# Splitting two projection weights once, in token block 2, for the last phase of a hybrid decoder block

## The chip, the core and the metric

The kernel runs on one core of a Trainium2 chip. The metric is the time of one execution in microseconds on the device, the median of several runs. A profile is one further execution, taken by the hardware profiler. The engines are TensorE (PE; its weight loads are PEld), VectorE (DVE), ScalarE (ACT), GpSimd (POOL) and SyncE (SP), which here issues the DMAs as one queue in order.

## What is computed

One decoder block on 2048 tokens of width 1024. An input projection feeds two branches, a causal convolution and an RWKV-7 recurrence; both are projected (`w_conv_out`, `w_rwkv_out`), merged by gates and projected once more (`w_out`).

```python
h = _rmsnorm(x, norm_g[l]) * (1.0 + scale[:, None, :]) + shift[:, None, :]
p = jnp.einsum('bsd,de->bse', h, w_in[l])
c_val, c_gate, c_og, ts, r_og, g_conv, g_rwkv = jnp.split(p, SPLITS, axis=-1)
y_conv = _conv_branch(c_val, c_gate, c_og, ..., w_conv_out[l])      # ... @ w_o
y_rwkv = _rwkv7_branch(ts, r_og, ..., w_rwkv_out[l])                # ... @ w_o
m = jax.nn.sigmoid(g_conv) * y_conv + jax.nn.sigmoid(g_rwkv) * y_rwkv
out = jnp.einsum('bsd,de->bse', m, w_out[l])
x = x + gate[:, None, :] * out
return _rmsnorm(x, final_g)
```

## The kernel before

The tokens are cut into four blocks of 512, the channels into eight tiles of 128. Every large matmul is made of three: a float32 operand is split into a high part (rounded to the type fp32r) and a low part (the rest), and the products high x high, high x low and low x high are summed (`mm3k`, L185). So each weight tile of 128 x 1024 (512 KB) is needed as two tiles of 512 KB.

`load_w` (L162) brings such a pair into the pool `w` of six buffers. If the pair is kept in DRAM, two DMAs fetch it (L168, L169). If not, the raw tile is loaded into a third buffer (L172), ACT casts it to the high part (L175), and DVE or POOL subtracts (L177). Pairs named in `KEPT`, the tiles of `w_in`, are then stored to DRAM for the later blocks (L181, L182). The last phase's output weight `w_o` is prepared apart: `ogate` (L147), called in token block 1, two weights in each of four groups, multiplies half a tile by the gate (POOL, L156), casts it (ACT, L157), subtracts (POOL, L158) and stores both halves (SP, L160). It works in the pool `hx` (L318), seven buffers of 128 x 512, which the normalisation of the next block's x (`xnorm`, L321) uses too, and with it the reading of the next block's input (`hprep`, L356).

The program has two parts. The first runs over the blocks (L859) and in each over four groups of heads: `group` (L560) holds the recurrence, with a triangular solve on POOL (L609, L611), its transposes on DVE (L637), the matmuls that read them (L641) and the state chain (L668 to L683); `conv` and `gates` (L746, L765) give PE projections to fill the chain's waits. The second part, the last phase, runs over the blocks again (L1030): `rproj` (L956) and `cproj` (L942) project the branches with w_ro and w_co through `project` (L733) and so `load_w`, eight tiles each and block; these 64 loads are raw, with `wcount[0] = -1000` (L964) giving their subtractions to DVE. Between them stand the output projection (L1059 to L1061), the next block's branch preparation (`osplit`, L927) and layer norm (`lnorm`, L984, whose statistics run L995, L1005, L1016 and whose values run L1024, L200 to L202, L1026, L912), and `finish` (L1071), the final norm with its run of one-column operations in `rsqrt` (L125 to L130).

The order on each engine is set by a scheduler that simulates the program when it is built (`schedule_with_timeline_sim`, L1135); `tc.high_priority` moves a few instructions ahead. On the chip each engine runs its own list in order.

Of the kernel before, what the change touches and what calls it, by code (L numbers as in the profile page):

```python
# [9 lines left out]
F32 = mybir.dt.float32  # L10
F32R = mybir.dt.float32r
I32 = mybir.dt.int32
AF = mybir.ActivationFunctionType
ALU = mybir.AluOpType
# [4 lines left out]
P = 128  # L19
D = 1024  # L20
KT = D // P
# [26 lines left out]
def lplan(t):  # L48
    n = {"c": 0, "g": 0}
    r = []  # L50
    for part in t.split():
        l = []
        for w in part:
            if w != "-":
                l.append(("1234" if w == "g" else w, n[w]))
                n[w] += 1
        r.append(l)
    return r
# [24 lines left out]
def hybrid_block(ctx: ExitStack, tc: tile.TileContext, x, vecs, convk, w2a2, final_g, ada, w_in, w_co, w_ro, w_o, crow, out,  # L83
                 seq=2048, groups=(0, 1, 2, 3), phase2=True, dbg=None):
    nc = tc.nc
# [6 lines left out]
    dp = ctx.enter_context(tc.tile_pool(name="dp", bufs=1, space=DRAM))  # L92
# [43 lines left out]
    wsrc = {"in": w_in, "co": w_co, "ro": w_ro, "o": {(cb, kh): w_o[cb, kh] for cb in range(4) for kh in range(2)}}  # L136
# [6 lines left out]
    kept = {}  # L143
# [3 lines left out]
    def ogate(n, half):  # L147

        back = kept.setdefault(("o", n), [dp.tile([P, KT, P], F32R, name=f"k{p_}_o{n[0]}_{n[1]}", tag=f"k{p_}_o{n[0]}_{n[1]}")
                                          for p_ in "hl"])  # L150
        hs = slice(half * 4, half * 4 + 4)
        st, gr, hi, lo = hx("w_st"), hx("w_gr"), hx("w_hi"), hx("w_lo")
        nc.sync.dma_start(st.rearrange("p (k n) -> p k n", k=4), wsrc["o"][n][:, hs, :])
        nc.sync.dma_start(gr[:, :256], grow_d[n[0] * 256:n[0] * 256 + 256].unsqueeze(0).broadcast_to([P, 256]))
        s4 = st.rearrange("p (k n) -> p k n", n=256)
        nc.gpsimd.tensor_tensor(out=s4, in0=s4, in1=gr[:, :256].unsqueeze(1).broadcast_to([P, 2, 256]), op=ALU.mult)  # L156
        nc.scalar.copy(hi.bitcast(F32R), st)  # L157
        nc.gpsimd.tensor_tensor(out=lo.bitcast(F32R), in0=st, in1=hi, op=ALU.subtract)  # L158
        for d_, s_ in zip(back, (hi, lo)):
            nc.sync.dma_start(d_[:, hs, :].bitcast(F32), s_.rearrange("p (k n) -> p k n", k=4))  # L160
# [152 lines left out]
    for g in range(4):  # L313
        s_ = c1.tile([P, 2, P], F32, name=f"S{g}")
# [3 lines left out]
    def hx(name):  # L318
        return xp.tile([P, TB], F32, name=name, tag="hx")

    def xnorm(b, tts=range(NTT)):  # L321
        for tt in tts:
            t0 = b * TB + tt * P
            ss = e2.tile([P, 8], F32, name="ss")
            xh = []
            for half in range(2):
                xt = hx("xt")
                nc.sync.dma_start(xt, x[t0:t0 + P, half * TB:half * TB + TB])
                nc.scalar.activation(hx("xsq"), xt, AF.Square, accum_out=ss[:, half:half + 1])
                xh.append(xt)  # L330
            vs, rs = ss[:, 2:3], ss[:, 3:4]
            nc.vector.tensor_tensor(out=vs, in0=ss[:, 0:1], in1=ss[:, 1:2], op=ALU.add)
            nc.vector.tensor_scalar(out=vs, in0=vs, scalar1=1.0 / D, scalar2=RMS_EPS, op0=ALU.mult, op1=ALU.add)
            rsqrt(rs, vs, e2, nc.vector, ss[:, 4:5])
            for kh in range(2):
                nc.vector.tensor_scalar(out=xh[kh], in0=xh[kh], scalar1=rs, scalar2=None, op0=ALU.mult)
                pt = pl.tile([P, 4, P], F32, name="late", tag="late")
                for i in range(4):
                    nc.tensor.transpose(pt[:, i, :], xh[kh][:, i * P:(i + 1) * P], ident)
                xo = hx("xTs").rearrange("p (a b) -> p a b", a=4)  # L340
                for i in range(4):
                    k = kh * 4 + i
                    nc.scalar.activation(xo[:, i, :], pt[:, i, :], AF.Identity, scale=g_col[:, k:k + 1],
                                         bias=shift_col[:, k:k + 1])
                nc.sync.dma_start(xT_dram[b][:, kh * 4:kh * 4 + 4, tt * P:(tt + 1) * P], xo)
# [10 lines left out]
    def hprep(b):  # L356
        h = ([], [])
        for k in range(KT):
            hf = hx("hf")
            nc.sync.dma_start(hf, xT_dram[b][:, k, :])  # L360
            hsplit(h, k, hf)
        return h
# [458 lines left out]
    def z_first(js):  # L821
        for j in js:
            z, bt = hx("z"), hx("zb")
            nc.sync.dma_start(z, o_dram[0][j])
            nc.sync.dma_start(bt, bv_dram[0][j])
            nc.gpsimd.tensor_tensor(out=z, in0=z, in1=bt, op=ALU.add)
            rt = hx("zr")
            nc.sync.dma_start(rt, ro_dram[0][j])
            nc.gpsimd.tensor_tensor(out=z, in0=z, in1=rt, op=ALU.mult)
            nc.sync.dma_start(z_dram[j], z)  # L830

    def lora_split(h):

        lf, ll, lx = hx("lora"), hx("lora_lo"), hx("lora_x")
        shifted(h, T_LORA, lf)
        nc.scalar.activation(lf[0:64], lf[0:64], AF.Tanh)
        lw = e1.tile([P, TB], F32R, name="lw", tag="lw")
        la = e1.tile([P, TB], F32R, name="la", tag="la")
        lo_, hi_ = slice(0, 64), slice(64, 128)
        for dst, sl, os_ in ((lw, lo_, hi_), (la, hi_, lo_)):  # L840
            nc.scalar.copy(dst[sl], lf[sl])
            nc.vector.tensor_tensor(out=ll[sl], in0=lf[sl], in1=dst[sl].bitcast(F32), op=ALU.subtract)
            nc.sync.dma_start(lx[os_], ll[sl])
            nc.scalar.copy(dst[os_], lx[os_])
        return lw, la
# [3 lines left out]
    def ada_steps():  # L849
        for k, _ in enumerate(ada_cols(srow, l3, "As", ASB, [((k, 8 + k), (mod[:, k:k + 1], mod[:, 8 + k:9 + k]))  # L850
                                                             for k in range(KT)])):
            ks, gs = slice(k, k + 1), slice(8 + k, 9 + k)
            nc.vector.tensor_tensor(out=shift_col[:, ks], in0=mod[:, ks], in1=ab[:, ks], op=ALU.add)
            nc.vector.tensor_tensor(out=g_col[:, ks], in0=mod[:, gs], in1=ab[:, gs], op=ALU.add)
            nc.vector.scalar_tensor_tensor(out=g_col[:, ks], in0=g_col[:, ks], scalar=1.0, in1=vc("norm_g", k),
                                           op0=ALU.add, op1=ALU.mult)
            yield

    for b in range(NB):  # L859
        h = hprep(b) if b else hprep0(x0, ada_steps())  # L860
        lora = lora_split(h)
        for g in groups:
            if b + 1 < NB:
                xnorm(b + 1, XN[g])
            else:
                z_first(ZN[g])
                if g < 3:
                    lnorm_first(g)
            if b + 1 < NB:
                todo = [(w, 2 * g + m) for w, m in (FIRST if b == 0 and g == 0 else NEXT)]  # L870
            else:
                todo = [wj for i in range(g, 4 if g < 3 else 5) if i == g or g == 3 for wj in lplan(LP)[i]]

            if b == 1:
                for _ in range(2):
                    n_ = later.pop(0)
                    for half in range(2):
                        ogate(n_, half)

            def fill(step, n=None):  # L880
                for _ in range(n or (FILL0[step] if b == 0 and g == 0 else 0)):
                    w, j = todo.pop(0)
                    if w == "c":
                        conv(b, h, j)
                    else:
                        gates(b, h, j, w)

            wcount[0] = WSH
            group(b, g, h, lora, fill)
            if b == 0 and g == GG:  # L890
                for _ in ada_cols(srow, l3, "As", ASB, [((16 + k, 17 + k), (hgate_col[:, k:k + 1], hgate_col[:, k + 1:k + 2]))
                                                        for k in range(0, KT, 2)]):
                    pass
                nc.vector.tensor_tensor(out=hgate_col, in0=hgate_col, in1=ab[:, 16:24], op=ALU.add)
                nc.vector.tensor_scalar(out=hgate_col, in0=hgate_col, scalar1=0.5, scalar2=None, op0=ALU.mult)
                nc.sync.dma_start(grow_d.rearrange("(n p) -> p n", p=P), hgate_col)
            wcount[0] = WDVE
            if todo:
                fill(0, len(todo))
# [75 lines left out]
    hl = ctx.enter_context(tc.tile_pool(name="hl", bufs=1, reuse_waits="tile"))  # L975
# [54 lines left out]
    for b in range(NB):  # L1030
# [7 lines left out]
        for tt in range(NTT):  # L1038
            xh = []
            for half in range(2):  # L1040
                n = 2 * tt + half
# [97 lines left out]
```

## Time and profile before

| | us |
|---|---|
| median of 3 runs (3077.19 to 3084.64) | 3080.32 |
| the profiled execution | 3079.25 |
| its span | 3077.6 |
| PE busy in the span | 2918.8 |
| DVE, ACT, POOL busy | 2182.2, 1059.7, 1161.0 |

Matmuls are pipelined, so PE's busy time counts overlapping operations once; where PE is not busy, it waits. A row of a group of instructions gives its line, engine, operation, the tiles (out<-in), the count, and durations. In a row of stretches of time (start:end, length) come the busy time of PE, PEld, DVE, ACT and POOL, each with the number of instructions in brackets, then the clock granted to PE as a share of full speed, the mean busy share of the 16 DMA engines, and GB/s.

### The profile page before, as it was taken

Reading aid. Unit: us, or ns where it says so; the run is one execution under the profiler, and the core shown is the slowest. Engines: PE = TensorE matmul, PEld = TensorE weight load, DVE = VectorE, ACT = ScalarE, POOL = GpSimd, SP = SyncE. Lnnn points to the kernel's source line nnn. Section 1 sums busy time; section 2 is a strip of 40 time slices with the busy share of each in tenths; the row PEclk is TensorE's granted clock in tenths of the full one; section 3 lists DMA queues with packets and bytes.
Section 4 is the critical chain, followed back from the end, with each engine's and each line's share of the span. In section 5 each row is a group of like instructions: output and inputs, shape, how many; then the busy total and the mean of one; then the engine's idle time right before and its main releaser. Section 6 shows DMA issues by size and latency. Waiting matters only on the chain.

```text
span 3077.6 us, 64859 instructions
## 1 busy us (share of the span) xinstructions
PE 2918.8 (95%) x25672; PEld 2759.5 (90%) x25672; DVE 2182.2 (71%) x4199; ACT 1059.7 (34%) x1919; POOL 1161.0 (38%) x1724
## 2 busy tenths in 40 slices
PE   6799998999999999999999999999989999699998
PEld 5789998999999999999999998999989888487888
DVE  7677877787777667777768586867699465877553
ACT  4424444343324241424232323233342224343421
POOL 3355554534343434241323326345445016533100
PEclk9989999999999999999999999999989999799999
DMA  8675767664757586555646567647448658766554
GB/s 301 221 239 192 262 206 268 229 235 136 249 160 229 163 269 218 178 167 173 204 149 217 181 202 247 192 142 224 139 146 263 207 187 287 246 205 220 198 182 161
DMA packets 343327, 638.41 MB, mean 207 GB/s; under 512 B 133424, under 2 KB 152176, under 8 KB 343024
## 3 DMA queue, kind: packets, MB, share of 16 engines
q1 hardware_dynamic: 343024, 634.27, 62.8%
q8 instruction: 202, 3.31, 0.4%
q14 instruction: 101, 0.83, 0.1%
HBM read 462.10 MB, written 170.92 MB: 206 GB/s over the span
## 4 chain that ended last, share of the span: by engine, by line
PE 62%; DVE 12%; DMA 10%; POOL 7%; issue 3%; ACT 2%; SPq 2%; DVEq 0%; POOLq 0%; ACTq 0%
PE ps_main L192 43%; PE aux L524 3%; DVE acc L761 2%; DMA w_st<-w_in_t 2%; POOL TT L611 2%; POOL itmp L609 2%; PE xo L673 2%; PE pout L1061 2%; PE pout L1060 2%; PE pout L1059 2%; DMA w_lo<-kl_in 1%; PE xo L668 1%; DMA w_gr<-grow_d 1%; PE xo L679 1%; PE late L695 1%
## 5 line engine op out<-in xcount | busy, mean ns | idle before, releaser
L192 PE MATMUL ps_main<-h_hi,w_hi 128*128 128x256 f32 x4608 | 961.4, 286 | 20.4 <-ACT w_hi L175 12.2
L192 PE MATMUL ps_main<-h_hi,w_lo 128*128 128x256 f32 x4608 | 962.3, 286 | 13.6 <-POOL w_lo L177 8.0
L192 PE MATMUL ps_main<-h_lo,w_hi 128*128 128x256 f32 x4608 | 956.7, 285 | 0.0
L192 PEld LDWEIGHTS ps_main<-h_hi,w_hi 128*128 128x128 f32 x4608 | 721.7, 190 | 30.4 <-ACT w_hi L175 13.3
L192 PEld LDWEIGHTS ps_main<-h_hi,w_lo 128*128 128x128 f32 x4608 | 719.7, 190 | 21.6 <-POOL w_lo L177 10.0
L192 PEld LDWEIGHTS ps_main<-h_lo,w_hi 128*128 128x128 f32 x4608 | 719.8, 190 | 5.2 <-issue 0.5
L761 DVE SCALAR_TENSOR_TENSOR acc<-u,ck,acc 128x512 f32<-128x512 f32 x928 | 698.6, 753 | 20.0
L175 ACT CAST w_hi<-w_st 128x1024 fp32r<-128x1024 f32 x135 | 141.5, 1048 | 368.9 <-DMA w_st<-w_in_t 151.6
L683 DVE SCALAR_TENSOR_TENSOR S<-xo,pe,Se 64x64 f32<-64x64 f32 x512 | 144.6, 282 | 128.1 <-PE xo L679 118.1
L609 POOL TENSOR_TENSOR itmp<-La,TT 128x126 f32<-128x126 f32 (+22 forms) x496 | 180.7, 364 | 141.9 <-DMA La<-dA 105.9
L611 POOL TENSOR_TENSOR TT<-TT,itmp 128x126 f32<-128x126 f32 (+22 forms) x496 | 190.5, 384 | 37.2
L177 DVE TENSOR_TENSOR w_lo<-w_st,w_hi 128x1024 fp32r<-128x1024 f32 x88 | 119.5, 1359 | 103.7 <-ACT w_hi L175 47.7
L177 POOL TENSOR_TENSOR w_lo<-w_st,w_hi 128x1024 fp32r<-128x1024 f32 x47 | 113.5, 2414 | 134.5 <-ACT w_hi L175 109.0
L665 ACT ACTIVATE Se<-S,pe 128x128 f32<-128x128 f32 x256 | 89.0, 395 | 209.1 <-DVE S L683 208.0
L524 PE MATMUL aux<-KR,BKz 128*128 128x128 f32 x1024 | 138.5, 285 | 13.5 <-ACT BKz L518 8.7
L547 POOL TENSOR_TENSOR vv<-rk,vv 128x512 f32<-128x512 f32 x32 | 44.0, 1374 | 284.2 <-ACT rk L546 268.8
L524 PEld LDWEIGHTS aux<-KR,BKz 128*128 128x128 f32 x1024 | 127.6, 198 | 16.1 <-ACT BKz L518 9.1
L675 DVE TENSOR_TENSOR uv<-xo,rn 64x256 f32<-64x256 f32 x128 | 53.7, 420 | 99.8 <-PE xo L673 98.2
L741 ACT ACTIVATE th<-ps_main 128x512 f32<-128x512 f32 x64 | 38.1, 595 | 210.5 <-PE ps_main L192 157.6
L526 DVE TENSOR_TENSOR As<-aux,maskA 128x512 f32<-128x512 f32 x128 | 87.0, 688 | 27.9 <-PE aux L524 26.4
L451 POOL TENSOR_TENSOR wlo<-wf,wl 64x128 fp32r<-64x128 f32 x64 | 37.4, 584 | 173.6 <-ACT wl L448 171.1
L773 ACT ACTIVATE th<-ps_main 128x512 f32<-128x512 f32 x64 | 38.2, 597 | 184.3 <-PE ps_main L192 179.7
(298 smaller groups left out, 5489.0 us busy)
## 6 DMA issues: line engine op xcount, KB each, us to landing
w_hi<-kh_in SPq DMA_DIRECT2D x219, 512.0 KB, 4.0
w_lo<-kl_in SPq DMA_DIRECT2D x219, 512.0 KB, 5.1
w_st<-w_in_t SPq DMA_DIRECT2D x73, 512.0 KB, 5.0
kh_in<-w_hi SPq DMA_DIRECT2D x71, 512.0 KB, 2.9
kl_in<-w_lo SPq DMA_DIRECT2D x71, 512.0 KB, 4.4
w_st<-w_ro_t SPq DMA_DIRECT2D x32, 512.0 KB, 4.0
w_st<-w_co_t SPq DMA_DIRECT2D x32, 512.0 KB, 3.6
w_hi<-kh_o SPq DMA_DIRECT2D x32, 512.0 KB, 3.7
```

Source lines behind the costliest of these rows:

```text
L175: nc.scalar.copy(hi, st)
L177: lo_eng.tensor_tensor(out=lo, in0=st, in1=hi.bitcast(F32), op=ALU.subtract)
L192: nc.tensor.matmul(ps[:, qs], ww[:, k, :], aa[k][:, qs], start=(k == 0 and t == 0 and q == 0), stop=(k == KT - 1 and t == 2 and q == ms - ...
L524: nc.tensor.matmul(pA[:, c // 2, es], BKz[:, hh, c // 2, es], KR[:, cc, es], start=(c == 0), stop=(c == 3), skip_group_check=True)
L526: nc.vector.tensor_tensor(out=Asb[:, hh, c4 * 4:c4 * 4 + 4, :].rearrange("p (a e) n -> p a (e n)", e=2), in0=pA, in1=flat(maskA).unsqueeze ...
L609: nc.gpsimd.tensor_tensor(out=tmp[:, :ni, :nt], in0=La[:, j:j + 1, j + 1:].broadcast_to([P, ni, nt]), in1=TT[:, :ni, j:j + 1].broadcast_to ...
L611: nc.gpsimd.tensor_tensor(out=TT[:, :ni, j + 1:], in0=TT[:, :ni, j + 1:], in1=tmp[:, :ni, :nt], op=ALU.add)
L665: nc.scalar.mul(Se[:, q, :], Sg[:, q, :], R[q]["pe"][:, c:c + 1])
L673: nc.tensor.matmul(xo[pr_, q, hs], As[q][pr_, hh, c, kcol(e)], XO[pr_, c, q, hs], start=(q == 0 and hh == 0), stop=(q == 1 and hh == 1), s ...
L683: nc.vector.scalar_tensor_tensor(out=Sg[hs, q, hs], in0=xo[hs, 2 + q, hs], scalar=R[q]["pe"][hs, c:c + 1], in1=Se[hs, q, hs], op0=ALU.mult ...
L761: nc.vector.scalar_tensor_tensor(out=acc if i + 1 < HALO else yj, in0=u[:, i:i + TB], scalar=ck[:, j, i:i + 1], in1=acc, op0=ALU.mult, op1 ...
L1059: nc.tensor.matmul(o_, mhi[kk][:, ts_], whi[:, k, :], start=first, stop=False, skip_group_check=True)
```

## The change

`keep` is `ogate` without the gate: half a raw tile of w_ro or w_co is loaded, cast on ACT, subtracted on POOL and stored as two halves in DRAM. It is called in token block 2, in every group for four of the sixteen tiles. `load_w` then finds the pair and fetches it, in all four blocks of the last phase.

```diff
+    pending = [(name, n) for name in ("ro", "co") for n in range(KT)]
+
+    def keep(name, n, half):
+        back = kept.setdefault((name, n), [dp.tile([P, KT, P], F32R, name=f"k{p_}_{name}{n}", tag=f"k{p_}_{name}{n}")
+                                           for p_ in "hl"])
+        hs = slice(half * 4, half * 4 + 4)
+        st, hi, lo = hx("w_st"), hx("w_hi"), hx("w_lo")
+        nc.sync.dma_start(st.rearrange("p (k n) -> p k n", k=4), wsrc[name][n][:, hs, :])
+        nc.scalar.copy(hi.bitcast(F32R), st)
+        nc.gpsimd.tensor_tensor(out=lo.bitcast(F32R), in0=st, in1=hi, op=ALU.subtract)
+        for d_, s_ in zip(back, (hi, lo)):
+            nc.sync.dma_start(d_[:, hs, :].bitcast(F32), s_.rearrange("p (k n) -> p k n", k=4))
...
+            if b == 2:
+                for _ in range(4):
+                    n_ = pending.pop(0)
+                    for half in range(2):
+                        keep(*n_, half)
```

Lines of the changed kernel are 13 higher from L162 on (18 from L880 on); the text uses the numbers of before. 64 casts of 128 x 1024 leave ACT and 64 subtractions leave DVE; 32 casts of 128 x 512 come to ACT and 32 subtractions to POOL. On SP, 64 loads of 512 KB are replaced by 128, and 96 DMAs of 256 KB come in.

The scheduler orders block 2 and all that follows anew. SP in block 2, group 3, before; dA and La carry the input of the triangular solve, kh_in and kl_in are kept w_in tiles:

```order
L168 DMA w_hi<-kh_in_7782 128x1024
L169 DMA w_lo<-kl_in_7783 128x1024
L595 DMA dA<-As 32x4x32 x8
L548 DMA bv_d_7_122<-vv 128x512
L168 DMA w_hi<-kh_in_7845 128x1024
L600 DMA La<-dA 64x1024 x2
```

and now (L169 and L173 are `keep`'s load and stores, L181 and L182 the w_in loads, L608 the dA stores):

```order
L181 DMA w_hi<-kh_in_7782 128x1024
L182 DMA w_lo<-kl_in_7783 128x1024
L173 DMA kh_co_20118<-w_hi 128x512
L169 DMA w_st<-w_co_t 128x512
L173 DMA kl_co_20119<-w_lo 128x512
L608 DMA dA<-As 32x4x32 x2
L173 DMA kh_co_21914<-w_hi 128x512
L169 DMA w_st<-w_co_t 128x512
L608 DMA dA<-As 32x4x32
```

Stores of halves, each waiting for a cast or a subtraction, and loads of the next halves now stand between the two w_in tiles and among the solve's own transfers. On POOL four of the 32 subtractions stand inside the solve of this group and six between it and the group's other work.

DVE in the last phase, at the passage from block 0's output to block 1's first projection, before; `rs` and `vs` are the final norm's columns, `mr` the first projection's result:

```order
L129 SCALAR_TENSOR_TENSOR rs_t<-rs_t,vs 128x1
L1080 SCALAR_TENSOR_TENSOR xt_31907<-xt_31907,rs_32399,fg 128x512
L1080 SCALAR_TENSOR_TENSOR xt_31909<-xt_31909,rs_32399,fg 128x512
L1075 TENSOR_SCALAR vs<-vs 128x1
L130 SCALAR_TENSOR_TENSOR rs_32418<-rs_t,rs_32418 128x1
L1074 TENSOR_REDUCE vs<-sq_31923 128x1
L177 TENSOR_TENSOR w_lo<-w_st,w_hi 128x1024
L202 SCALAR_TENSOR_TENSOR y_31741<-th,y_31741 128x512
L962 SCALAR_TENSOR_TENSOR mr_32472<-rth,ps_main 128x512
```

and now (L215, L930, L980 and L1044 are L202, L912, L962 and L1026 of before):

```order
L215 SCALAR_TENSOR_TENSOR y_32046<-th,y_32046 128x512
L1092 TENSOR_REDUCE vs<-sq_32211 128x1
L1044 TENSOR_TENSOR y_32043<-y_32043,ct 128x512
L1093 TENSOR_SCALAR vs<-vs 128x1
L930 TENSOR_TENSOR u_lo<-y_32040,u_hi 128x512
L1093 TENSOR_SCALAR vs<-vs 128x1
L980 SCALAR_TENSOR_TENSOR mr_32760<-rth,ps_main 128x512
L215 SCALAR_TENSOR_TENSOR y_32049<-th,y_32049 128x512
L125 TENSOR_SCALAR rs_32687<-vs 128x1
```

The first `mr` stood behind the first y (L202) and a run of final-norm operations; now seven of the eight y stand before it, and the one-column run (L125 to L130) behind it.

PE at the same passage, before; `pout` is the output projection, `prl` the layer norm's last matmul, `m_hi` the first matmul of the next projection:

```order
L1060 MATMUL pout<-w_lo,o_hi_31592 128x256
L1061 MATMUL pout<-w_hi,o_lo_31591 128x256
L1016 MATMUL prl<-dg,ones 128x512
L192 MATMUL ps_main<-m_hi_31644,w_hi 128x512
L192 MATMUL ps_main<-m_lo_31652,w_hi 128x512
```

and now (L1077 to L1079 are L1059 to L1061, L1034 is L1016):

```order
L1078 MATMUL pout<-w_lo,o_hi_31888 128x256
L1079 MATMUL pout<-w_hi,o_lo_31887 128x256
L1034 MATMUL prl<-dg,ones 128x512
L1078 MATMUL pout<-w_lo,o_hi_31884 128x256
L1079 MATMUL pout<-w_hi,o_lo_31883 128x256
```

`prl` was the last before the projection; now 140 matmuls of the output projection follow it.

## The prediction

> **What bounds the kernel now.** I read the page's head and its 40 slices first, then the busy time by token block and by stretch of the last phase, then what TensorE waited for.
>
> ```profile
> span 3077.6 us, 64859 instructions
> ...
> PE 2918.8 (95%) x25672; PEld 2759.5 (90%) x25672; DVE 2182.2 (71%) x4199; ACT 1059.7 (34%) x1919; POOL 1161.0 (38%) x1724
> ...
> PE   6799998999999999999999999999989999699998
> ...
> PEclk9989999999999999999999999999989999799999
> ```
>
> PE is full nearly everywhere; its dips are the start and two slices in the last phase, where the granted clock falls too. The next rows split the time behind block 0: block 1, block 2, block 3, last phase. The columns are start:end and length, busy time of PE, PEld, DVE, ACT and POOL, granted clock, DMA share and GB/s.
>
> ```profile
> 664.00:1247.00 583.00, 573.04 (x5611) 556.75 (x5611) 424.82 (x856) 195.07 (x378) 220.60 (x394) 1.00 0.64 205
> 1247.00:1828.00 581.00, 576.65 (x5633) 560.93 (x5632) 421.76 (x861) 190.32 (x367) 183.85 (x364) 1.00 0.56 181
> 1828.00:2440.00 612.00, 596.10 (x5779) 575.51 (x5778) 447.33 (x851) 194.62 (x348) 269.44 (x421) 0.98 0.61 194
> 2440.00:3078.00 638.00, 581.03 (x3257) 496.74 (x3256) 395.84 (x709) 209.04 (x374) 171.11 (x116) 0.95 0.63 212
> ```
>
> Block 2, which gets the new work, leaves PE idle for 4.4 us of 581 (581.00 - 576.65). The last phase, which loses work, leaves 57.0 us of 638. Where these lie:
>
> ```profile
> 2440.00:2450.00 10.00, 7.27 (x28) 5.76 (x28) 6.50 (x14) 5.53 (x11) 0.00 (x0) 0.66 0.77 249
> 2540.00:2600.00 60.00, 55.68 (x416) 53.33 (x415) 29.58 (x53) 24.07 (x54) 36.61 (x28) 0.94 0.88 308
> 2600.00:2690.00 90.00, 59.30 (x222) 44.55 (x221) 79.10 (x121) 34.51 (x53) 52.71 (x35) 0.82 0.73 244
> ...
> 2730.00:2830.00 100.00, 92.77 (x577) 82.05 (x576) 76.71 (x131) 42.87 (x83) 45.74 (x30) 0.98 0.74 253
> 2830.00:2880.00 50.00, 49.06 (x209) 38.64 (x208) 40.43 (x59) 24.23 (x31) 13.31 (x8) 1.00 0.53 168
> 2880.00:3078.00 198.00, 186.94 (x1182) 167.89 (x1180) 84.23 (x209) 44.03 (x99) 0.00 (x0) 0.98 0.53 180
> ```
>
> More than half of it, 30.7 us, lies in 2600 to 2690, the passage from block 0's output to block 1's projections, at a clock of 0.82; DVE is busy there for 79.1 of 90 us. The 11.1 us after 2880 are the kernel's tail and stay. What PE itself waited for in the last phase (total, times, longest):
>
> ```profile
> PE ps_main L192 <- DVE rs L125: 10.8, 1, 10.8
> PE ps_main L192 <- ACT w_hi L175: 10.8, 2, 6.2
> PE ps_main L192 <- DVE w_lo L177: 8.5, 3, 4.1
> PE ps_main L192 <- DVE mr L962: 4.3, 2, 3.7
> PE pout L1059 <- DMA w_hi<-kh_o: 3.9, 1, 3.9
> ```
>
> So the splits made in the last phase (L175, L177) end 19.3 us of PE's waits, and a run of DVE's small operations (L125) another 10.8.
>
> **What leaves the last phase.** All 64 splits of w_ro and w_co go. The rows below are L177 alone on DVE in the passage and in the whole phase (a record is missing), then L175 on ACT.
>
> ```profile
> 2600.00:2690.00 90.00, 13.56 (x10) 0.00 (x0) 0.82 0.73 244
> ...
> 2440.00:3078.00 638.00, 85.82 (x63) 0.00 (x0) 0.95 0.63 212
> ```
>
> ```profile
> 2440.00:3078.00 638.00, 65.05 (x62) 0.95 0.63 212
> ```
>
> DVE loses 85.8 us and ACT 65.1; most was hidden under PE. Each weight also took three of the six `w` buffers (raw, high, low) and now takes two, so three weights can be loaded ahead instead of two.
>
> In the passage the direct gain is 13.6 us of DVE's time, where DVE is the engine waited for. The new order adds to it: the layer norm's last matmul (L1016) stands 140 output matmuls earlier, and DVE's small operations (L125 to L130) behind the values that PE waits for, so part of the 10.8 us goes as well. And idle PE time costs clock: at 0.82 the 59.3 us of work contain 59.3 x 0.18 = 10.7 us. Idle and clock together, 41.4 us, are the most that can go; nothing is the least. The transfers stand between, since each of the ten weights in this stretch now moves 1 MB instead of 0.5.
>
> ```profile
> 2540.00:2690.00 150.00, 114.99 (x635) 97.88 (x634) 108.68 (x173) 58.58 (x107) 89.32 (x63) 0.87 0.79 269
> ```
>
> ```profile
> 2560.00:2570.00 10.00, 6.36 (x27) 5.62 (x28) 1.20 (x2) 1.51 (x5) 7.66 (x7) 0.66 1.03 404
> 2640.00:2650.00 10.00, 10.00 (x45) 7.91 (x44) 10.00 (x12) 3.43 (x5) 7.98 (x5) 1.00 1.00 369
> 2950.00:2960.00 10.00, 10.00 (x45) 8.04 (x44) 3.37 (x4) 1.05 (x1) 0.00 (x0) 1.00 1.00 345
> ```
>
> The 150 us at 269 GB/s are 40.4 MB; ten more half megabytes make 45.6 MB. With the DMA engines at a share of 1.00 the trace shows 345 to 404 GB/s. At 345 the 45.6 MB take 132 us, so the passage can lose 18 us before the queue decides it. I take **18 us** for the passage, the nearest such row at its careful end.
>
> The Trainium skill, "DMA: Bandwidth & Descriptors", section "Where 436 GB/s comes from", sets a core's limit at about 358 GB/s between HBM and SBUF; by it the same bytes take an estimated 127 us and the passage could lose 23. The windows with 369 and 404 GB/s lie above that figure, so the trace does not bear it out as a ceiling.
>
> The other stretches: 2730 to 2880 has 7.2 + 0.9 = 8.1 us of idle PE, and DVE is again the busier engine; I take half, **4 us** (0 to 8). In 2540 to 2600 PE waits for an output weight (kh_o, 3.9 us) at a DMA share of 0.88, and the w_co loads before it double: **+1 us** (0 to +4.3, its idle time again). At 2440 to 2450 a split stood before a step of the state chain (2.7 us of idle); now that chain's last steps stand with fewer matmuls between them. **0** (-2.7 to +2.7).
>
> **What block 2 gets.** 16 weights in 32 halves: each a load of 256 KB, a cast on ACT, a subtraction on POOL and two stores of 256 KB, 96 DMAs on SP. Block 1 already does this for the gated w_o, 16 halves with one more POOL operation each, through the same buffers:
>
> ```profile
> L157 ACT CAST w_hi<-w_st x16: 618/620/623, 807.7 to 1169.9; 128x512 fp32r<-128x512 f32 x16
> ```
>
> ```profile
> L158 POOL TENSOR_TENSOR w_lo<-w_st,w_hi x16: 1271/1296/1305, 808.4 to 1170.6; 128x512 fp32r<-128x512 f32 x16
> ```
>
> So ACT gets 32 x 0.62 = 19.8 us (busy 190 of 581), POOL 32 x 1.30 = 41.5 us (184 of 581), and the queues 25.2 MB, 43 GB/s beside 181. All of it lies under PE's matmuls as long as no queue is held up. Block 1, with 32 such POOL operations, has 10.0 us of idle PE against block 2's 4.4, and is 2 us longer. I take **+4 us**, between these two differences, rounded up; the ends are 0 (work is only added, so no gain) and 41.5, all of POOL's time in the open.
>
> The place to fear is group 3 of block 2, where four of POOL's subtractions now stand inside the triangular solve (L609, L611) and six just ahead of it. The last transpose of the solve's result and the matmul that reads it:
>
> ```profile
> 1797.57 0.30 DVE L637 STREAM_TRANSPOSE T<-As 32x128 f32<-32x128 f32 x1 [0.20 <-DMA As<-dT]
> ```
>
> ```profile
> 1837.46 2.04 PE late L641 x64
> ```
>
> PE comes to it 40 us later, since it stands behind fill matmuls; ten subtractions are 13.0 us. The cover holds; without it they would cost those 13.
>
> **The sum.** Against the profiled execution's own 3079.25 us (span 3077.6 and 1.65 around it; 1.07 below the median of 3080.32): -18 - 4 + 1 + 0 + 4 = -17, **3062 us**.
>
> **The rivals.** *The queue takes it.* If the passage's bytes move only at the 308 GB/s of 2540 to 2600, 45.6 MB take 148 us and the passage gains 2: 3079.25 - 2 - 4 + 1 + 4 = 3078, no change. For it: shares of 0.88 and 1.00 around the passage. Against: 2600 to 2690 has a share of only 0.73, and loads three weights ahead can spread.
>
> *All of the idle time goes.* DVE's small operations are slow because of POOL:
>
> ```profile
> 2607.34 1.18 DVE L128 TENSOR_TENSOR rs_t<-rs 128x1 f32<-128x1 f32 x1
> 2608.45 0.14 DVE L125 TENSOR_SCALAR rs<-vs 128x1 int32<-128x1 int32 x1
> 2608.56 1.22 DVE L129 SCALAR_TENSOR_TENSOR rs_t<-rs_t,vs 128x1 f32<-128x1 f32 x1
> 2609.70 0.15 DVE L128 TENSOR_TENSOR rs_t<-rs 128x1 f32<-128x1 f32 x1
> ```
>
> ```profile
> 2608.47 10.47 POOL L1024 TENSOR_TENSOR y<-y,rl 128x512 f32<-128x512 f32 x8
> ```
>
> Operations on one column take 0.14 us or 1.2, the latter about one of POOL's eight operations (10.47 / 8 = 1.31). In the new order the run of small operations stands behind most of what follows those eight (L202, L1026), so it may escape them. Then the passage loses 36 of its 41.4 us and the next one 7, with 2 in block 2: 3079.25 - 36 - 7 + 2 = 3038. Against: POOL still has the next block's additions (L931, L932) then, and the bytes at 404 GB/s would still need 113 us.
>
> The Trainium skill, "SBUF — State Buffer", section "SBUF: two separate sides", says that POOL and a DVE operation with two SBUF inputs take a shared pair of ports under an exclusive lock, the loser waiting for the whole instruction. The trace agrees: the two-input rows show 1.2 us and the one-input row 0.14. By that rule the run goes back to about 0.15 us an operation wherever POOL is idle, which is this rival; it also lets the 32 new subtractions hold DVE in block 2, where DVE has 159 us of slack.
>
> *Slower: SP holds back the weights of block 2.* SP is one queue in order, and each store of a half waits there for ACT or POOL, ahead of the next w_in loads. Block 1 shows the wait and what it did to PE:
>
> ```profile
> SPq L160 <- ACT w_hi L157: 52.7, 15, 6.2
> ```
>
> ```profile
> PE ps_main L192 <- DMA w_lo<-kl_in: 2.9, 2, 2.5
> ```
>
> ```profile
> 1805.05 24.94 PE ps_main L192 x210
> ```
>
> The last row is a stretch of plain projections in the chain of waits. Twice as many halves, with up to fifteen rows between two weight loads, could make holds longer than PE's cover: two loaded weights of 48 matmuls each, at 24.94 / 210 = 0.119 us, are 11.4 us. If 16 weights come 2.5 us late each: 3079.25 - 21 + 40 = 3098. Against: 3.5 us a hold on average, under that cover, and block 2 is as full in PE now as before.
>
> That the change does nothing is excluded: the order shows the 64 casts and 64 subtractions gone.
>
> **How the numbers follow.** Forecast 0.56 (its own range 3050 to 3073), no gain 0.18, all of the idle time 0.14, slower 0.12. The range leaves out the last and half of the large gain: **3040 to 3083**. A measurement of this kernel tells about 0.2% (6 us) from no change; faster than that: 0.53 of the forecast, 0.14, and 0.02 of the no-gain case, 0.69; within it 0.17; slower 0.12 and 0.02, 0.14.
>
> **What would show it.** In the changed profile: no L175 or L177 in the last phase; the passage of 2600 to 2690 shorter, with PE's idle time near 15 us and DMA at 300 GB/s or more; PE's waits for w_hi and w_lo naming transfers (kh_ro, kl_co), if any; block 2 within 4 us of 581, with PE idle below 9. Waits of PE for kl_in in block 2 of tens of us would prove the slower rival; a passage as long as now with a DMA share near 1.00 the first one; and a start of the last phase 10 us later would break my term for block 2.

## The result and the profile after

| | us |
|---|---|
| before, median of 5 runs beside the changed kernel's | 3080.32 |
| after, median of 5 runs (3058.53 to 3071.97) | 3066.17 |
| ratio, 95% interval | 0.9948 (0.9932 to 0.9963) |
| the profiled execution after, its span | 3067.37, 3065.6 |

The kernel became 14.2 us faster; 17 were forecast, and the time lies 4 us above the forecast. Two terms missed by more than that, in opposite directions. The page after, head, busy times and slices:

```profile
span 3065.6 us, 65067 instructions
...
PE 2922.3 (95%) x25672; PEld 2762.5 (90%) x25672; DVE 2103.1 (69%) x4135; ACT 1010.4 (33%) x1887; POOL 1200.7 (39%) x1756
...
PE   6799998999999999999999999999999998899998
...
PEclk9989999999999999999999999999999999999999
```

The slice of the last phase where PE stood at 6 and its clock at 7 (2616 to 2693 us) is gone: two slices now stand at 8 there, the clock at 9. DVE has 79 us less. To see where the time went, the two traces are cut at the same places of the program: the last matmul of part one (it reads h, the normalised x), and the first output matmul of blocks 0, 1 and 2. The timeline of before at these places (start, us, engine, line, operation):

```profile
2439.69 0.36 PE L192 MATMUL ps_main<-h_hi,w_lo 128*128 128x256 f32 x1
2547.80 0.28 PE L1059 MATMUL pout<-w_hi,o_hi 128*128 128x256 f32 x1
2737.74 0.28 PE L1059 MATMUL pout<-w_hi,m_hi 128*128 128x256 f32 x1
2886.68 0.28 PE L1059 MATMUL pout<-w_hi,o_hi 128*128 128x256 f32 x1
```

And after:

```profile
2452.32 0.40 PE L205 MATMUL ps_main<-h_hi,w_lo 128*128 128x256 f32 x2
2563.68 0.36 PE L1077 MATMUL pout<-w_hi,o_hi 128*128 128x256 f32 x1 [3.85 <-DMA w_hi<-kh_o]
2733.16 0.41 PE L1077 MATMUL pout<-w_hi,m_hi 128*128 128x256 f32 x2
2872.79 0.28 PE L1077 MATMUL pout<-w_hi,o_hi 128*128 128x256 f32 x1
```

Part one ends at 2452.4 (the second of the two matmuls in that row), 12.7 us later. The four stretches behind it were 108.1, 189.9, 148.9 and 190.9 us and are 111.3, 169.5, 139.6 and 192.8: +3.2, -20.4, -9.3 and +1.9, in all 24.6 us less. So the last phase gave more than forecast (21), and part one took back half of it (forecast 4).

PE's waits in the last phase, after:

```profile
PE ps_main L205 <- DVE mr L980: 6.2, 3, 4.2
PE pout L1077 <- DVE cth L966: 5.1, 1, 5.1
PE pout L1077 <- DMA w_hi<-kh_o: 3.8, 1, 3.8
PE pvar L1023 <- POOL qs L1020: 2.7, 1, 2.7
PE ps_main L205 <- DVE xt L1085: 2.6, 1, 2.6
```

The waits for the splits (10.8 and 8.5) and for the run of DVE's small operations (10.8) are gone; one wait of 5.1 us, for cth, is new.

Block 2 and what follows it, by stretches (columns as in the prediction); before first, then after:

```profile
1240.00:1840.00 600.00, 595.65 (x5841) 1.00 0.57 182
1840.00:2439.70 599.70, 583.80 (x5632) 0.98 0.61 194
```

```profile
1240.00:1840.00 600.00, 586.63 (x5676) 0.99 0.68 219
1840.00:2452.40 612.40, 597.89 (x5789) 0.98 0.61 196
```

These rows show PE alone with the clock, the DMA share and GB/s. PE's idle time in 1240 to 1840 rose from 4.4 to 13.4 us, and 165 matmuls fewer were done there (5841 - 5676).

### The profile page after: what moved, and what is told of

It reads as the page before. It is cut to its first block, busy times and chain, and to the rows that moved or that the text cites. A ratio compares the mean times of both kernels' runs of the same rounds, so it can differ in the third digit from the quotient of the medians.

```text
span 3065.6 us, 65067 instructions
## 1 busy us (share of the span) xinstructions
PE 2922.3 (95%) x25672; PEld 2762.5 (90%) x25672; DVE 2103.1 (69%) x4135; ACT 1010.4 (33%) x1887; POOL 1200.7 (39%) x1756
## 4 chain that ended last, share of the span: by engine, by line
PE 49%; DMA 17%; DVE 13%; POOL 10%; issue 4%; SPq 4%; ACT 3%; POOLq 0%; DVEq 0%; ACTq 0%
PE ps_main L205 32%; POOL TT L624 4%; POOL itmp L622 3%; PE aux L537 3%; DMA w_st<-w_in_t 2%; DVE acc L774 2%; DMA xt<-x_in 2%; PE pout L1077 2%; PE pout L1079 2%; PE pout L1078 2%; DMA La<-dA 2%; DMA w_lo<-kl_in 2%; PE xo L686 1%; DMA w_st<-w_co_t 1%; SPq L635 1%
## 5 line engine op out<-in xcount | busy, mean ns | idle before, releaser
L624 POOL TENSOR_TENSOR TT<-TT,itmp 128x126 f32<-128x126 f32 (+22 forms) x496 | 189.9, 383 | 37.1
L190 POOL TENSOR_TENSOR w_lo<-w_st,w_hi 128x1024 fp32r<-128x1024 f32 x47 | 113.4, 2413 | 135.8 <-ACT w_hi L188 115.9
L188 ACT CAST w_hi<-w_st 128x1024 fp32r<-128x1024 f32 x71 | 74.3, 1047 | 195.5 <-DMA w_st<-w_in_t 148.6
L681 PE MATMUL xo<-S,KR 128*128 128x128 f32 x512 | 96.4, 284 | 6.4 <-DVE S L696 6.0
L786 ACT ACTIVATE th<-ps_main 128x512 f32<-128x512 f32 x64 | 38.2, 597 | 185.9 <-PE ps_main L205 175.7
L683 DVE TENSOR_TENSOR XO<-xo,XO 128x256 f32<-128x256 f32 x128 | 53.6, 419 | 66.2 <-PE xo L681 55.5
L949 POOL TENSOR_TENSOR ot<-ot,bt 128x512 f32<-128x512 f32 x24 | 34.1, 1420 | 165.3 <-DMA bt<-bv_d 148.6
```

The lines of the kernel that those rows point to most:

```text
L188: nc.scalar.copy(hi, st)
L190: lo_eng.tensor_tensor(out=lo, in0=st, in1=hi.bitcast(F32), op=ALU.subtract)
L624: nc.gpsimd.tensor_tensor(out=TT[:, :ni, j + 1:], in0=TT[:, :ni, j + 1:], in1=tmp[:, :ni, :nt], op=ALU.add)
L681: nc.tensor.matmul(xo[:, q, :], R[q]["KR"][:, cc, es], Sg[:, q, :], start=(q == 0), stop=(q == 1), skip_group_check=True)
```

## The experiments

Each kernel was run in turn with the kernel before on one chip, and each ratio is to those runs (medians of before 3075.96, 3076.89 and 3075.4 in the three sets of four). The ratios on record differ from the quotients of the medians by up to 0.001 (3 us). The table cuts each profiled execution, to within 0.1 us, at the places above: the end of part one, then the stretches to the first output matmul of blocks 0, 1, 2 and to the end.

| kernel | part one ends | to block 0's | to block 1's | to block 2's | to the end | ratio (interval) |
|---|---|---|---|---|---|---|
| before | 2439.7 | 108.1 | 189.9 | 148.9 | 190.9 | 1 |
| after | 2452.4 | 111.3 | 169.5 | 139.6 | 192.8 | 0.9948 (0.9932 to 0.9963) |
| e1 kept, not used | 2449.1 | 106.8 | 179.8 | 152.5 | 190.9 | 1.0014 (1.0000 to 1.0028) |
| e2 pairs, no split | 2432.5 | 112.7 | 167.3 | 139.7 | 192.2 | 0.9912 (0.9898 to 0.9926) |
| e3 one tile | 2435.1 | 107.4 | 166.7 | 140.8 | 192.4 | 0.9898 (0.9880 to 0.9915) |
| e4 kept in the last phase | 2433.2 | 126.0 | 178.1 | 139.5 | 191.7 | 0.9987 (0.9975 to 0.9998) |
| e5 no subtraction | 2449.7 | 109.2 | 166.9 | 139.9 | 192.1 | 0.9948 (0.9931 to 0.9965) |
| e6 and one store | 2432.8 | 112.8 | 168.5 | 139.2 | 190.9 | 0.9943 (0.9922 to 0.9963) |
| e7 cast twice | 2435.1 | 115.7 | 164.6 | 147.7 | 192.3 | 0.9943 (0.9924 to 0.9961) |
| e8 subtraction on DVE | 2459.7 | 107.3 | 172.2 | 139.5 | 192.3 | 0.9997 (0.9984 to 1.0011) |
| e9 raw stores | 2465.2 | 108.2 | 173.0 | 139.3 | 192.4 | 1.0025 (1.0014 to 1.0036) |
| e10 no stores | 2426.3 | 108.2 | 158.3 | 144.0 | 192.3 | 0.9898 (0.9879 to 0.9918) |
| e11 two blocks | 2456.3 | 109.5 | 166.9 | 139.4 | 192.3 | 0.9995 (0.9981 to 1.0008) |
| e12 w_ro alone | 2455.5 | 119.0 | 178.5 | 145.6 | 192.2 | 1.0046 (1.0028 to 1.0064) |

The profiled executions of e6 and e10 were 13 and 14 us faster than the medians of their kernels, at a granted clock of 0.984 and 0.985 where the others had 0.974 to 0.982; an estimate for their part one at the median is 11 us later (14 x 2430 / 3045). For these two the ratio counts, not the first column.

How far can the first column be trusted? To the end of part one, the instructions stand in the same order on PE, DVE, ACT and POOL in before, e2, e3, e4 and e7, and these five end it at 2432.5 to 2439.7 us (mean 2435.1). So 7 us there can be chance. After and e1 share an order too and end it at 2452.4 and 2449.1. By these seven, the new work costs part one 9 to 20 us, and 15.6 between the two means. The other kernels have other orders from about 1390 us on.

### The two halves apart

**e1**: the work in block 2 stays, the last phase splits its weights as before.

```diff
-        back = kept.get((name, n))
+        back = None if name in ("ro", "co") else kept.get((name, n))
```

> The 16 weights are split and stored in token block 2 as in the changed kernel, but the last phase ignores the stored pairs and splits for itself as before. This is the added work alone. Theory A (block 2's work costs about 10 us, more than the 4 of the prediction, and the last phase gains about 22 to 24): 3090 us, with the extra time in token block 2. The prediction's own term: 3084. Rival B (block 2's work is free; the last phase gains only about the 14 us measured): 3080.

Measured 3081.0, ratio 1.0014: by the number alone, rival B. But part one ends 9.4 us later than before, and the last phase, split for split the same work in a new order, is 7.9 us shorter (630.0 for 637.9). So the price by the whole time, 4, hides a larger one in part one. In its passage PE waits for the splits on DVE, a wait that is gone in the changed kernel (L190 is L177 of before):

```profile
PE ps_main L205 <- DVE w_lo L190: 14.7, 6, 7.0
```

**e2**: nothing in block 2; the last phase fetches kept pairs of w_in instead of splitting.

```diff
+        if name in ("ro", "co"):
+            back = kept[("in", n + (0 if name == "ro" else 8))]
```

> No splitting in token block 2; the last phase fetches a stored pair of w_in tiles for each of the 64 w_ro and w_co weights (same sizes and transfers as the changed kernel; the two projections are computed with other weights). This is the removed work alone. Theory A: 3080 - 22 to 24 = 3056 to 3058 us. Rival B: 3066, like the changed kernel.

Measured 3051.99, ratio 0.9912: 27 us, or 24 by the medians, as theory A had it. Against the change's 0.9948 this prices the work in block 2 at 0.0036, some 11 us (about 5 to 17, an estimate from the two intervals).

**e3**: as e2, with one tile for both parts, so the bytes of the raw load.

```diff
+        if name in ("ro", "co"):
+            hi = whl.tile([P, KT, P], F32R, name="w_hi", tag="w", bufs=WB)
+            nc.sync.dma_start(hi.bitcast(F32), kept[("in", n + (0 if name == "ro" else 8))][0].bitcast(F32))
+            return hi, hi
```

> As the run before, but one stored tile of 512 KB is fetched for each weight and used as both parts (the low part is left out), so the last phase moves 33.6 MB less. If the doubled bytes hold up the passages of the last phase (the prediction's limit of 18 us by the queue), this is faster than the run with pairs by some 10 us or more: about 3045. If DVE and POOL's own order set the passages, it is within 4 us of it: 3053 to 3058.

Measured 3045.78, ratio 0.9898. That is the time that the theory of the bytes had named, 6 us under e2, though the two intervals overlap. But the passage from block 0's output to block 1's takes 166.7 us with half the bytes and 167.3 with all. **The doubled bytes do not set it.** What differs is the stretch before it, 107.4 us for 112.7: there e2 waits 6.0 us for the output weight kh_o, and e3 does not.

**e7**: the kernel before with a second cast on ACT in place of DVE's subtraction, so that ACT's chain, the raw loads and three buffers a weight stay.

```diff
+            if name in ("ro", "co"):
+                nc.scalar.copy(lo, st)
+            else:
+                lo_eng.tensor_tensor(out=lo, in0=st, in1=hi.bitcast(F32), op=ALU.subtract)
```

> The kernel before, where the last phase's 64 subtractions on DVE are replaced by a second cast on ACT into the same tile (the low part of w_ro and w_co is wrong): raw loads, three buffers for a weight and the cast in the chain stay, DVE loses 86 us and ACT gains 65. Theory A (DVE's time is what bounds the passages): most of the 27 us of the run with stored pairs and no split comes, the last phase takes 615 to 622 us instead of 638, 16 to 23 us under the kernel before. Theory B (the three buffers, so only two weights ahead, and the raw load with its cast bound them): the last phase takes 630 to 638, 0 to 8 us under.

Measured 3058.27, ratio 0.9943. The passage takes 164.6 us, as short as in e2, though the raw loads, the casts and the third buffer are still there: with the subtractions off DVE they do not hold it at 189.9. The edit is also a new order, and e1's new order alone brings the passage to 179.8, so the 25 us are not the price of DVE's subtractions alone. PE's waits in e7's last phase:

```profile
PE ps_main L195 <- DVE mr L965: 8.2, 2, 5.5
PE pout L1062 <- DMA w_hi<-kh_o: 7.2, 1, 7.2
PE ps_main L195 <- ACT w_hi L175: 6.5, 2, 3.5
PE ps_main L195 <- DVE rs L125: 2.5, 1, 2.5
```

The 6.5 us for ACT's cast all lie in the passage, and the wait for DVE's run of small operations has shrunk from 10.8 to 2.5. Theory A held for the passage, and the last phase fell to 620.4, as it said. The next stretch stays at 147.7 (148.9 before, 139.7 in e2). What PE waits for there in e7 is not the cast:

```profile
PE ps_main L195 <- DVE mr L965: 2.8, 1, 2.8
PE ps_main L195 <- DVE rs L125: 2.5, 1, 2.5
```

These are DVE's operations again. Why this stretch needs the stored pairs stays open.

### What costs part one

**e5** leaves POOL's subtraction out (both stored halves are the high part); **e6** leaves out one store as well.

```diff
-        st, hi, lo = hx("w_st"), hx("w_hi"), hx("w_lo")
+        st, hi = hx("w_st"), hx("w_hi")
...
-        nc.gpsimd.tensor_tensor(out=lo.bitcast(F32R), in0=st, in1=hi, op=ALU.subtract)
-        for d_, s_ in zip(back, (hi, lo)):
+        for d_, s_ in zip(back, (hi, hi)):      # e5
+        for d_, s_ in zip(back[:1], (hi,)):     # e6
```

> The changed kernel with POOL's 32 subtractions in block 2 left out; both stored halves are the high part, so the low part of w_ro and w_co is wrong, and the stores and the last phase's loads stay as they are. Theory P (POOL's 41.5 us of work in block 2 is what costs part one some 10 us, by holding DVE and the triangular solve): PE idle between 1240 and 1840 us falls from 13.4 to about 5, part one ends near 2440, and the time is 24 to 28 us under the kernel before. Theory Q (the 96 extra DMAs and the waits on SP's queue cost it): idle stays at 11 to 13, part one ends near 2450, and the time is 14 to 17 under the kernel before.

> As the run with the subtractions left out, and one of the two stores of each half left out as well: 64 DMAs of 256 KB in block 2 instead of 96; the last phase loads the one stored tile twice, so its bytes stay. Theory P: no further change against the run with both stores (within 4 us). Theory Q: a third of block 2's loss goes, 3 to 5 us under the run with both stores, PE idle between 1240 and 1840 near 9.

Measured 3060.31 (0.9948) and 3059.26 (0.9943): both ratios are the change's own. The windows of e5:

```profile
1240.00:1840.00 600.00, 595.43 (x5783) 1.00 0.69 224
1840.00:2449.70 609.70, 591.37 (x5721) 0.97 0.59 193
```

The idle time in 1240 to 1840 fell to 4.6, as theory P had it, but part one still ended at 2449.7. Behind 1840 PE is idle for 18.3 us, where the kernel before has 15.9 and the changed kernel 14.5, so idle time in block 2 does not account for the loss. P and Q both failed as stated.

**e8**: block 2's subtraction on DVE (`nc.gpsimd` to `nc.vector` in `keep`).

> The changed kernel with block 2's 32 subtractions on DVE instead of POOL, the same results. Theory P: the half tiles take DVE about 0.7 us each, 22 us of its slack, POOL's 41.5 us go, and most of block 2's loss with them: PE idle between 1240 and 1840 at 5 to 8, 18 to 24 us under the kernel before. Theory Q: like the change itself, 13 to 17 under.

Measured 3074.31, ratio 0.9997: the gain is gone, and both theories missed. Part one ends at 2459.7, though POOL lost 42 us of work there. Moving the work to the engine with slack was worse.

**e9**: the halves are stored as loaded, with no cast and no subtraction; **e10**: cast and subtracted, but not stored, and the last phase as in e2.

```diff
-        st, hi, lo = hx("w_st"), hx("w_hi"), hx("w_lo")
-        nc.scalar.copy(hi.bitcast(F32R), st)
-        nc.gpsimd.tensor_tensor(out=lo.bitcast(F32R), in0=st, in1=hi, op=ALU.subtract)
-        for d_, s_ in zip(back, (hi, lo)):
+        st = hx("w_st")                         # e9
+        for d_, s_ in zip(back, (st, st)):
```

```diff
-        for d_, s_ in zip(back, (hi, lo)):      # e10
-            nc.sync.dma_start(d_[:, hs, :].bitcast(F32), s_.rearrange("p (k n) -> p k n", k=4))
...
-        back = kept.get((name, n))
+        back = kept.get(("in", n + (0 if name == "ro" else 8)) if name in ("ro", "co") else (name, n))
```

> The changed kernel with neither cast nor subtraction in block 2: each half tile is loaded and stored twice as it is, so the 96 DMAs stay on SP, which waits for no engine any more, and one buffer of hx is taken instead of three (the stored parts of w_ro and w_co are both the raw weight). The yardstick is the run with stored pairs and no split, 27 us under the kernel before. Theory D (the transfers themselves cost block 2, by the bytes beside the recurrence's own DMAs): 15 to 18 us under the kernel before, PE idle between 1240 and 1840 us at 4 to 7, little else than in the run without subtractions. Theory H (it costs because SP, buffers and the chain of DVE are held up by the new work of ACT and POOL): 23 to 28 under, PE idle there 3 to 4.5.

> The changed kernel without the 64 stores: the halves are loaded, cast and subtracted in block 2 and then dropped; the last phase fetches kept pairs of w_in in place of w_ro and w_co (so it uses other weights, with the same bytes). Theory D (the transfers cost): 21 to 25 us under the kernel before. Theory H (the engines' new work costs, not the stores): 12 to 19 under, PE idle between 1240 and 1840 at 9 or more.

Measured 3082.1 (1.0025) and 3044.65 (0.9898), e9 slower than before and e10 31 us under it, so both runs lie outside both theories. The stretches of e9, then of e10, with PE, PEld, DVE, ACT and POOL:

```profile
1240.00:1840.00 600.00, 580.08 (x5633) 561.28 (x5631) 421.75 (x854) 193.94 (x371) 187.01 (x367) 0.98 0.64 213
```

```profile
1240.00:1840.00 600.00, 594.92 (x5797) 579.02 (x5797) 439.95 (x886) 218.06 (x414) 226.16 (x400) 1.00 0.60 197
```

e10 has all the work of ACT and POOL (218 and 226 us busy) and 5.1 us of idle PE; it is no slower than e2. e9 has none of that work and 19.9 us of idle PE, and loses all of the gain. **In these two runs the loss goes with the stores, not with the engines' work.** What PE waits for in e9 from 1240 to the end of part one:

```profile
PE xo L679 <- DVE S L694: 8.0, 7, 3.2
PE late L652 <- DVE T L648: 7.1, 2, 6.6
PE aux L535 <- ACT BKz L529: 4.6, 1, 4.6
```

These are the recurrence's own results (its state S and the transposes T of its solve) that come late; waits for w_in weights are small (4.9 us). How the stores make them late was not separated: the transfers beside the recurrence's DMAs, SP's order around them, or the whole new order that the scheduler makes once they are there. No run holds the order fixed, so a costly order that merely came with the stores is not excluded. The loss does not follow their number: e6 has half of the change's stores and the change's ratio, e9 has as many as the change and loses 24 us more (1.0025 - 0.9948, of 3075).

### Other places for the work

**e4**: no work in block 2; the last phase stores each pair when its first block has split it (`KEPT = ("in", "ro", "co")` in the kernel before).

> The kernel before with KEPT = in, ro, co: the last phase's block 0 still splits its 16 weights, and stores the pairs for blocks 1 to 3; nothing in token block 2. Theory A (block 2's work costs 10): the passages gain nearly as in the changed kernel, 2 to 4 us less for block 0, and the 10 us are not paid: 3058 to 3062 us, faster than the changed kernel. Rival B (block 2's work is free): 3068, slower than the changed kernel.

Measured 3071.01, ratio 0.9987. Theory A missed; rival B is near in its number, but e2 speaks against its reason. Part one has no new work and ends at 2433.2. The first stretch, which now splits and stores 16 MB, takes 126.0 us for 108.1, and the passage gains only to 178.1.

**e11**: two weights in each group of blocks 2 and 3; **e12**: w_ro alone in block 2, w_co split in the last phase.

```diff
-            if b == 2:
-                for _ in range(4):
+            if b >= 2:                          # e11
+                for _ in range(2):
```

```diff
-    pending = [(name, n) for name in ("ro", "co") for n in range(KT)]
+    pending = [(name, n) for name in ("ro",) for n in range(KT)]     # e12
...
-                for _ in range(4):
+                for _ in range(2):
```

> The changed kernel with the same work spread over blocks 2 and 3, two weights a group instead of four. If the cost comes of the crowding (several halves held in a row, theory H), part one loses less than half as much: 18 to 24 us under the kernel before. If every half costs the same wherever it stands (theory D, or DVE and POOL's lock), 12 to 17 under, like the change.

> The changed kernel that keeps w_ro alone, two weights a group in block 2; w_co is loaded raw and split in the last phase as before. Of the last phase's 24.7 us that part goes which w_ro's 32 splits cost, and half of block 2's price. The passage after block 0 projects w_ro and w_co of block 1 in turn, so I expect half of both by either theory: 5 to 12 us under the kernel before. If w_ro's splits are those that stood on the path, 16 to 22 under, better than the change.

Measured 3070.93 (0.9995) and 3090.09 (1.0046). Both missed all that was expected of them. Thinner spreading did not help, so crowding alone does not explain the price. In e12 half of the work cost part one as much as all of it (2455.5), and the last phase kept 635.2 of 637.9 us. No version that computes the same beat the change.

## Why the prediction came out right

**Passage, -18 (2600 to 2690): -22.3, with the wrong reason.** Cut as the prediction cut it, from the last output matmul of block 0, the passage took 135.7 us before and takes 113.4 now. The size came from the queue at 345 GB/s. e3 has half of the bytes and the same passage, e7 the old bytes and the same passage: the transfers did not limit it. DVE did, by its order and its splits: e1, in a new order with all splits, has 123.6 by this cut, 12.1 less than before, and the other 10.2 go with the splits for which PE waits there (and with one more order). The other signs that were named for it came: no split in the last phase, and from the last output matmul of block 0 to the first of block 1 less idle time (135.00 - 104.30 = 30.7 us before, 12.4 after; near 15 forecast) at 326 GB/s (300 or more forecast). PE, clock, DMA share and GB/s, before and then after:

```profile
2602.00:2737.00 135.00, 104.30 (x398) 0.86 0.65 211
```

```profile
2619.00:2733.00 114.00, 101.61 (x406) 0.93 0.91 326
```

The queue also ran faster than the 345 GB/s that I had taken; two stretches of 10 us after:

```profile
2800.00:2810.00 10.00, 9.96 (x41) 7.14 (x40) 6.18 (x13) 4.86 (x7) 6.72 (x6) 1.00 1.04 410
2660.00:2670.00 10.00, 10.00 (x43) 7.74 (x42) 3.92 (x7) 2.43 (x4) 2.31 (x2) 1.00 1.04 405
```

What is left there is named by the waits above for mr, qs and xt: operations of DVE and POOL. What went besides the splits bears on the rival in which all idle time goes. DVE's run of one-column operations lasted from 2606.3 to 2659.1 before; after, its first and last rows are

```profile
2635.38 0.20 DVE L125 TENSOR_SCALAR rs<-vs 128x1 int32<-128x1 int32 x2
...
2654.57 0.23 DVE L130 SCALAR_TENSOR_TENSOR rs<-rs_t,rs 128x1 f32<-128x1 f32 x2
```

19.4 us instead of 52.8. Much of the difference is other work that stood among them: the 40 one-column operations themselves were busy for 23.5 us and are now for 9.4. Of the 36 with two inputs, 16 took about 1.2 us before, and four take more than 1 us now; most take 0.15. POOL was busy for 66% of the run before and is for 60% now, but its work leaves a pause of 6.95 us, in which the last 16 of them fall, each about 0.15 us:

```profile
2658.47 1.39 POOL L1011 TENSOR_TENSOR ys<-ys,y 128x512 f32<-128x512 f32 x1 [6.95 <-DMA y<-y_d]
```

That is as the Trainium skill's rule has it ("SBUF — State Buffer", section "SBUF: two separate sides"). The prediction read more into its rows: it gave 1.2 us to the two-input operations, but its fourth row is one of 0.15, and beside POOL's eight operations eight of 15 such took 1.2 and seven 0.15. The rival's price, 36 us, was too high; the slow operations that it named were real, and PE's wait of 10.8 us for them is gone.

**2730 to 2880, -4: -9.3**, 7.1 of its 8.2 us of idle time and 2.3 us of PE's busy time, not half. Half was a guess, and why nearly all went is open. PE waited there for DVE's operations (4.3 us for mr, 2.3 for m_lo), and e7, which takes the subtractions off DVE, gained only 1.2.

**2540 to 2600 +1, and the junction 0: +5.1 together** (162.3 us from the end of part one to the last output matmul of block 0, now 167.4), but not by the wait for kh_o, which stayed at 3.8 us (3.9 before). There is a new wait of 5.1 us, for cth. It looks like the slow operations of DVE beside POOL again, in another place. DVE's subtractions o_lo before, and then after, with POOL's sums of the layer norm that now stand beside them:

```profile
2543.32 3.49 DVE L912 TENSOR_TENSOR o_lo<-mr,o_hi 128x512 fp32r<-128x512 f32 x5
```

```profile
2561.77 6.76 DVE L930 TENSOR_TENSOR o_lo<-mr,o_hi 128x512 fp32r<-128x512 f32 x4
2568.45 0.68 DVE L966 SCALAR_TENSOR_TENSOR cth<-cth,ps_main 128x512 f32<-128x512 f32 x1
```

```profile
2559.58 10.08 POOL L1011 TENSOR_TENSOR ys<-ys,y 128x512 f32<-128x512 f32 x6
```

Before, five took 3.49 us; after, four take 6.76, and cth stands behind them. The new order put POOL's sums beside them. No run moved those sums alone, so this cause is read from the rows, not tested.

**Block 2, +4: the step that failed; it is +12.7 in the two profiles and 11 by e2.** The engines' work was priced well (ACT 19.8 us for 19.8, POOL 42.6 for 41.5), and e10, which has all of it, loses nothing:

```profile
L170 ACT CAST w_hi<-w_st 128x512 fp32r<-128x512 f32 x32 | 19.8, 619 | 85.5 <-DMA w_st<-w_co_t 45.5 <-DMA w_st<-w_ro_t 23.3 <-issue 6.6
L171 POOL TENSOR_TENSOR w_lo<-w_st,w_hi 128x512 fp32r<-128x512 f32 x32 | 42.6, 1333 | 99.5 <-ACT w_hi L170 91.7 <-DMA dA<-As 6.3 <-DMA kl_co<-w_lo 1.4
```

The stores had no term of their own: the queues were taken as free beside 181 GB/s, under the condition that no queue is held up. What showed in its place is a loss that is there with the stores (e9) and not without them (e10); its mechanism stays open. The rival on SP's queue was right that SP would wait for the new casts and subtractions (1240 to 1840 us):

```profile
SPq L181 <- PE ps_main L205: 186.3, 50, 11.1
SPq L173 <- ACT w_hi L170: 46.1, 24, 4.2
...
SPq L173 <- POOL w_lo L171: 7.9, 13, 1.3
```

But PE waits for w_in weights only 3.5 us from 1240 to the end of part one. In e9, where SP waits for no engine before a store, only some 18 us for transfers, the loss is larger. PE idle for more than 9 us in block 2 and a start of the last phase 10 us later were named as what would break this term, and both came (13.4 and 12.7).

So the forecast came within 3 us of the change because errors cancelled, which is luck. The two gains came out 9.6 us larger than forecast (4.3 and 5.3). The losses came out larger too: 4.1 us before the passage, 1.9 in the tail, which had no term, and 8.7 in block 2. The median differs from the profiled executions by another 2.

One reading at the prediction's start was wrong without weight in the sum: of its two slices with a low clock only one lies in the last phase, the other (2231 to 2308 us) in block 3.

## What to carry to other kernels

Price the waited-for engine first, and test it by giving its work to another engine: e3 and e7 cleared the bytes, which had been taken for the limit, and pointed to DVE. Work put beside a dependent chain is not priced by the busy time of the engines that do it; run it once with its stores and once without, before choosing a place for it. Where a scheduler orders the program, each edit is also a new order, worth about 10 us in a stretch here (e1), so cut the traces at the same events and compare the stretches. Look first for kernels that share an order over a stretch: they show how much of a difference is chance, here up to 7 us for part one.

## What was not expected of the hardware

- DVE and POOL, each with operations of two inputs from SBUF, run in step: DVE's o_lo takes 0.69 us alone and 1.69 beside POOL (6.76 / 4), POOL's sum 1.30 alone (behind 2747 us of the changed kernel) and 1.68 (10.08 / 6). Both slow down, and one of each takes 1.69 us, less than the sum of the two, 1.99.
- The 16 DMA engines moved 405 and 410 GB/s in stretches of 10 us, above the 358 that the Trainium skill ("DMA: Bandwidth & Descriptors", section "Where 436 GB/s comes from") gives for a core.
- Runs of one and the same kernel differ, in part with the granted clock: e10 took 3030.68 us at 0.985 and 3045.72 at 0.980. The clock is not all of it: two runs of e1 at 0.980 took 3072.72 and 3088.43.
